# Stick-breaking values by pairs of heads in the two column halves of TensorE, with transposed outputs, and the group norm by partition sums right behind the heads

## The chip, the cores and the metric

The kernel runs on one core of one Trainium2 chip. The metric is the time of one execution on the device in microseconds (us), the median of several; less is better. All times below are us unless marked ns. The engines are TensorE (PE; its weight loads are shown apart as PEld), VectorE (DVE), ScalarE (ACT), GpSimd (POOL) and SyncE (SP), which issues the DMAs.

## The reference

Two transformer blocks, one behind the other, on 512 tokens of 1024 channels in fp32. The first block's mixer has four groups of 256 channels: a short convolution (group 0), a block-sparse attention with compressed tokens (NSA, group 1), a latent attention (MLA, group 2) and a stick-breaking attention of four heads of 64 (group 3). Each group is normalised by itself and all four go through one output projection. Only group 3 is touched:

```python
def stick_breaking_mixer(q, k, v):                       # 4 heads of 64
        z = jnp.einsum('bqhd,bkhd->bhqk', q_blk, k) * scale
        strict = kpos < (t0 + arange(Q_BLOCK))           # key before query
        log_1m = where(strict, log_sigmoid(-z), 0.0)
        rem = cumsum(log_1m, axis=3, reverse=True) - log_1m
        a = where(strict, exp(log_sigmoid(z) + rem), 0.0)
        return einsum('bhqk,bkhd->bqhd', a, v)
...
y = concatenate([y_a, y_b, y_c, y_d]).reshape(B, S, N_GROUPS, GROUP_WIDTH)
y = rms_norm(y, out_norm_w.reshape(N_GROUPS, GROUP_WIDTH))
x = x + y.reshape(B, S, D) @ w_out
```

## The kernel before

Everything stays in on-chip memory except the weights, which stream in on SP's queue (`wraw`, L268). A product of two fp32 matrices is mostly done as three matmuls on split operands (high and low part, L184, L185, L186; ACT makes a high part, L276 for weights and L192 for data, DVE the low part, L277 and L193). Some smaller products run as plain fp32 matmuls; each of those leaves two records in the trace.

A head of the stick-breaking group (`sb_head`, L960) has three steps. `first` makes the transposed logits, keys on partitions and queries along the free axis, causal part only, in three PSUM banks (L981, L982), and turns them into log terms: three passes of ACT (L987 to L989), one of DVE (L990), a causal select of POOL (L974), and a split (L192, L193, names `sbLh`, `sbLl`). `second` adds the running sums by matmuls with triangles (L1002) and takes the exponential (ACT, L1006, name `sba`; POOL's select again). `third` multiplies by the values: for each of the ten causal pairs of a query tile and a key tile, the 128x128 block of `sba` is the stationary operand and 64 columns of `svN` move (L1014), and ACT copies the result, tokens on partitions, into `yN` (L1016).

The loop over heads calls `second` of head h, `first` of head h+1, `third` of head h, and between them takes steps of a side generator: the projections of the values, of the NSA keys and values (L184 to L186 into `kvN`), and the hidden layer of the compressed tokens (`compress_hidden`), whose operand `cB` is made from `cv0` and `cv1` (DVE L1243, a split by ACT and DVE into `cB`) and consumed by the matmuls L1252 and L1254. `cv1` needs rows shifted by a DMA (L700). Behind the heads stand `group_stats` (squares with sums on ACT L853, a power on POOL L227, scaling on DVE L857) and `compress_out` (POOL copies `Tc` L1118, fed by a round trip to memory L1101, L1108; a norm with POOL's power `crs`, L227; DVE `ckn` L1290; PE L1295). The transposes of `yN` into `yT6` and `yT7` come later (`group_out`, L866). Lines L453 to L468 (`token_rs`, `token_bcast`) are the norm by partition sums that the convolution group has: four matmuls with a vector of ones, a power on POOL, diagonal tiles on DVE (L464), one matmul that spreads the factor over all partitions (L466), a copy, two multiplications.

The Python order is not the order of the program: a scheduler takes all instructions with their dependences and fixes one order for each engine. Each engine then works strictly in its order and waits where an operand is not there.

Of the kernel before, what the change touches and what calls it, by code (L numbers as in the profile page):

```python
# [22 lines left out]
P = 128  # L23
# [126 lines left out]
class Kern:  # L150
# [427 lines left out]
    def mixers1(self):  # L578
# [73 lines left out]
        with tc.tile_pool(name="mx", bufs=1) as mp:  # L652
# [28 lines left out]
            def ev_qv(t, b):  # L681
                nc.scalar.activation(qN[:, t, :], b[:, :256], AF.Copy, scale=nm.rs[:, t:t + 1])
                nc.vector.tensor_scalar(svN[:, t, :], b[:, 256:512], nm.rs[:, t:t + 1], None, op0=OP.mult)
            ySB = self.T(mp, [P, NT, 256], F32, "yN", 2)
            ncv = self.T(mp, [P, NT, 352], F32, "ncv")
            gN = self.T(mp, [P, NT, 12], F32, "ng", 1)
            xs = self.T(self.drp, [P, 8, S], F32, "xs", 1)
# [36 lines left out]
            def side2():  # L724
# [12 lines left out]
                        tc.keep_in_program_order(nc.sync.dma_start(xs[:, k, :], self.x[k]))  # L737
                        yield
                yield from self.along(self.conv(mp, nm, w), itertools.chain(self.mla_stats(mp, ncv), store()))
                self.group_out(ySB, 3, "pT")  # L740
                cq = self.mla_trans(mp, ncv)
                yield
                yield from self.mla_proj(mp, ncv, cq, st)
                yield from self.along(self.conv_gate(nm, w, st), self.mla_rope(mp, ncv, st["mla"]), 2)
                norm = self.conv_norm(st["acc"])
                for h in range(4):
                    hd.append(self.mla_head(h, st["mla"]))
                    yield
# [19 lines left out]
                    yield  # L768
            hd = []
            self.fq.append(side())  # L770
            heads = [self.sb_head(mp, h, sq[h], sk[h], svN, ySB) for h in range(4)]
            self.fill(10)
            heads[0][0]()
            self.fill(16)
            for h in range(4):
# [5 lines left out]
                    heads[h + 1][0]()  # L781
                heads[h][2]()
                self.fill(6)
            self.dbg("ySB", ySB)
            self.yH = [None] * 8
            for k in (2, 3):
                self.yT[k] = self.T(mp, [P, S], F32, f"yT{k}")
            self.drain()
            g2 = side2()
            self.fq = [self.weave(self.compress_out(mp, st), g2, 2), g2]  # L790
            self.group_stats(mp, ySB, 3)
            n = self.nsa_prep(mp, qN, st["kvN"])
            self.fill(8)
            self.fill(2)
            while "g" not in st:
                self.fill(1)
# [160 lines left out]
        self.nc.tensor.matmul(out, q[h][:, qs], k.hi[:, ks], start=True, stop=False)  # L957
        self.nc.tensor.matmul(out, q[h][:, qs], k.lo[:, ks], start=False, stop=True)  # L958

    def sb_head(self, mp, h, q, k, svN, ySB):  # L960

        nc = self.nc
        st = {}
# [3 lines left out]
        def R(kt, t, q0=None):  # L967
            o = 384 if kt == 3 else 0
            q0 = kt if q0 is None else q0
            return t[bank[kt]][:, o + (q0 - kt) * P: o + (NT - kt) * P]  # L970

        def causal(a, i):
            for o in ([0, 384] if i == 1 else [0]):
                nc.gpsimd.affine_select(out=a[:, o:o + P], in_=a[:, o:o + P], pattern=[[1, P]], compare_op=OP.is_gt,  # L974
                                        fill=0.0, base=0, channel_multiplier=-1)

        def first():
            st["z"] = z = [self.ps('L'), self.ps('L'), self.ps('pT')]
            for kt in (0, 1, 3, 2):
                ks = slice(kt * P, (kt + 1) * P)  # L980
                nc.tensor.matmul(R(kt, z), k.hi[:, ks], q[:, kt * P:S], start=(kt != 3), stop=False, skip_group_check=True)  # L981
                nc.tensor.matmul(R(kt, z), k.lo[:, ks], q[:, kt * P:S], start=False, stop=True, skip_group_check=True)  # L982
            st["hi"], st["lo"] = [], []
            for i in range(3):
                n = widths[i]
                e = self.T(mp, [P, 512], F32, "sbe", 3)[:, :n]
                nc.scalar.activation(e, z[i][:, :n], AF.Abs)  # L987
                nc.scalar.activation(e, e, AF.Exp, scale=-1.0)
                nc.scalar.activation(e, e, AF.Ln, bias=1.0)  # L989
                nc.vector.scalar_tensor_tensor(e, z[i][:, :n], 0.0, e, op0=OP.max, op1=OP.add)  # L990
                causal(e, i)
                hl = self.hl(mp, [P, 512], "sbL", 3)
                self.split(hl[:, :n], e)
                st["hi"].append(hl.hi)
                st["lo"].append(hl.lo)

        def second():
            z = st["z"]
            for kt in range(NT):
                for m, j in [(self.trir, kt)] + [(self.negr, j) for j in range(kt + 1, NT)]:  # L1000
                    for src in (st["hi"], st["lo"]):
                        nc.tensor.matmul(R(kt, z, j), m, R(j, src), start=False, stop=True, skip_group_check=True)  # L1002
            st["a"] = []
            for i in range(3):
                a = self.T(mp, [P, 512], F32, "sba", 3)
                nc.scalar.activation(a[:, :widths[i]], z[i][:, :widths[i]], AF.Exp)  # L1006
                causal(a, i)
                st["a"].append(a)

        def third():  # L1010
            ov = self.ps('o')[:, :256].rearrange("p (t d) -> p t d", t=NT)
            for qt in range(NT):
                for kt in range(qt + 1):
                    nc.tensor.matmul(ov[:, qt, :], R(kt, st["a"], qt)[:, :P], svN[:, kt, h * 64:(h + 1) * 64],  # L1014
                                     start=(kt == 0), stop=(kt == qt))
            nc.scalar.activation(ySB[:, :, h * 64:(h + 1) * 64], ov, AF.Copy)  # L1016
        return first, second, third

    def conv(self, mp, nm, w):
# [35 lines left out]
                nc.vector.tensor_add(acc, acc, sq)  # L1055
        yield from self.tproj_g(nm.H, w, [(0, 256)], ev_b)

    def conv_norm(self, acc):
        rs = self.token_rs(acc, S, 1.0 / 256, "L")
        yield  # L1060
        R = self.token_bcast(rs, S, "L")
        yield
        for c in range(2):
            self.nc.vector.tensor_mul(self.yT[c], self.yT[c], R)
        yield

    def nsa_norms(self, mp, qN, kvN):
# [993 lines left out]
```

## Time and profile before

| | before |
|---|---|
| median of 3 runs | 1604.54 (1604.54 to 1604.95) |
| the profiled execution | 1605.0, its span 1603.2 |
| mean granted clock of TensorE | 0.997 |
| PE busy | 1586.2, 99% of the span |
| DVE, ACT, POOL busy | 927.7, 678.8, 52.5 |

The span runs from the first to the last instruction in the trace; the execution's own time holds 1.8 more around it. The four heads and the work woven between them lie within the first 122 us of the span; the two tiles of transposes that the change removes are at 169 and 170. Behind that, the rest of the first block and all of the second are the same code before and after.

### The profile page before, as it was taken

The numbers are of one execution on the slowest core, as the hardware profiler recorded it, in microseconds if no ns is written. First come the engines' busy times: TensorE is split into PE (matmuls) and PEld (weight loads), VectorE is DVE, ScalarE is ACT, GpSimd is POOL, SyncE is SP. The second block draws the span as 40 slices with busy tenths as digits, with TensorE's granted clock in tenths as the row PEclk, the third lists the DMA queues.
The fourth block names the chain that finished last, engine by engine and source line by source line (L and its number), as shares of the span: only waits on it lengthen the run. The fifth ranks groups of instructions, "written<-read, shape, count | busy, mean of one in ns | idle before, by whom it ended". The sixth has DMA issues, their size and how long they took to land.

```text
span 1603.2 us, 20825 instructions
## 1 busy us (share of the span) xinstructions
PE 1586.2 (99%) x8075; PEld 1332.7 (83%) x8075; DVE 927.7 (58%) x1597; ACT 678.8 (42%) x1170; POOL 52.5 (3%) x99
## 2 busy tenths in 40 slices
PE   9999999999999999999999999999999999999998
PEld 7888878888888888888898777888988888888886
DVE  6666885644324433476666665674767556436662
ACT  5776654544213333344343366362544333213332
POOL 0121010000000000000000000000000000000000
PEclk9999999999999999999999999999999999999999
DMA  5243121223222232232222211333323233323331
GB/s 179 76 131 124 53 99 40 79 94 104 92 99 99 92 102 95 88 92 60 76 64 72 84 45 67 119 101 109 121 92 105 82 103 94 104 92 99 97 119 53
DMA packets 108134, 148.15 MB, mean 92 GB/s; under 512 B 7903, under 2 KB 58884, under 8 KB 108036
## 3 DMA queue, kind: packets, MB, share of 16 engines
q1 hardware_dynamic: 107892, 146.72, 28.6%
q8 instruction: 63, 1.03, 0.3%
q14 instruction: 35, 0.29, 0.1%
q10 hardware_dynamic: 144, 0.11, 0.0%
HBM read 142.31 MB, written 4.20 MB: 91 GB/s over the span
## 4 chain that ended last, share of the span: by engine, by line
PE 94%; DVE 4%; ACT 1%; POOL 1%; issue 1%; POOLq 0%; DVEq 0%; ACTq 0%
PE mm L184 27%; PE mm L186 27%; PE mm L185 26%; PE lv L1642 2%; PE o L912 1%; PE o L1685 1%; PE pT L901 1%; PE o L1815 1%; PE L L957 1%; PE pT L1792 1%; PE L L958 1%; DVE wlo L277 1%; PE o L184 0%; PE o L186 0%; PE o L185 0%
## 5 line engine op out<-in xcount | busy, mean ns | idle before, releaser
L277 DVE TENSOR_TENSOR wlo<-wraw,whi 128x1024 fp32r<-128x1024 f32 (+4 forms) x267 | 310.3, 1163 | 436.0 <-ACT whi L276 424.4
L276 ACT ACTIVATE whi<-wraw 128x1024 fp32r<-128x1024 f32 (+4 forms) x267 | 269.8, 1011 | 539.0 <-PE mm L185 472.6
L184 PE MATMUL mm<-H4h,whi 128*128 128x512 f32 x147 | 59.2, 403 | 0.0
L184 PE MATMUL mm<-H6h,whi 128*128 128x512 f32 x147 | 58.4, 401 | 0.4 <-ACT H6h L195 0.4
L184 PE MATMUL mm<-H7h,whi 128*128 128x512 f32 x147 | 58.3, 397 | 0.0
L488 DVE TENSOR_TENSOR x<-mm,x 128x512 f32<-128x512 f32 x72 | 48.8, 686 | 16.2 <-PE mm L186 15.7
L184 PE MATMUL mm<-H5h,whi 128*128 128x512 f32 x147 | 57.9, 394 | 0.0
L186 PE MATMUL mm<-H6h,wlo 128*128 128x512 f32 x147 | 57.7, 393 | 0.0
L185 PE MATMUL mm<-H7l,whi 128*128 128x512 f32 x147 | 57.7, 392 | 0.0
L185 PE MATMUL mm<-H6l,whi 128*128 128x512 f32 x147 | 57.7, 392 | 0.0
L186 PE MATMUL mm<-H4h,wlo 128*128 128x512 f32 x147 | 57.6, 392 | 0.0
L186 PE MATMUL mm<-H7h,wlo 128*128 128x512 f32 x147 | 57.4, 391 | 0.0
L185 PE MATMUL mm<-H4l,whi 128*128 128x512 f32 x147 | 57.3, 390 | 0.0
L186 PE MATMUL mm<-H5h,wlo 128*128 128x512 f32 x147 | 57.3, 390 | 0.0
L185 PE MATMUL mm<-H5l,whi 128*128 128x512 f32 x147 | 57.3, 390 | 0.0
L184 PE MATMUL mm<-H0h,whi 128*128 128x512 f32 x139 | 55.3, 398 | 0.0
L184 PE MATMUL mm<-H3h,whi 128*128 128x512 f32 x139 | 55.2, 397 | 0.0
L184 PE MATMUL mm<-H2h,whi 128*128 128x512 f32 x139 | 55.1, 397 | 0.0
L184 PE MATMUL mm<-H1h,whi 128*128 128x512 f32 x139 | 54.8, 394 | 0.0
L185 PE MATMUL mm<-H2l,whi 128*128 128x512 f32 x139 | 54.6, 392 | 0.0
L186 PE MATMUL mm<-H0h,wlo 128*128 128x512 f32 x139 | 54.5, 392 | 0.0
L186 PE MATMUL mm<-H2h,wlo 128*128 128x512 f32 x139 | 54.5, 392 | 0.0
(1300 smaller groups left out, 4190.4 us busy)
## 6 DMA issues: line engine op xcount, KB each, us to landing
wraw<-ffn_w_dram SPq DMA_DIRECT2D x64, 512.0 KB, 3.6
wraw<-w_up_dram SPq DMA_DIRECT2D x88, 256.0 KB, 2.9
wraw<-w_in_dram SPq DMA_DIRECT2D x35, 512.0 KB, 3.5
wraw<-w_down_dram SPq DMA_DIRECT2D x22, 512.0 KB, 3.6
wraw<-w_mem_kv_dram SPq DMA_DIRECT2D x16, 512.0 KB, 3.7
wraw<-w_in_dram SPq DMA_DIRECT2D x52, 128.0 KB, 2.3
wraw<-w_in_dram SPq DMA_DIRECT2D x22, 256.0 KB, 2.9
wraw<-cmp_w_dram SPq DMA_DIRECT2D x8, 512.0 KB, 4.7
```

Of the source, the lines that this page charges most:

```text
L184: mm(out, a.hi, b.hi, start=start, stop=False, skip_group_check=skip)
L185: mm(out, a.hi, b.lo, start=False, stop=False, skip_group_check=skip)
L186: mm(out, a.lo, b.hi, start=False, stop=stop, skip_group_check=skip)
L276: nc.scalar.activation(hi, raw, AF.Copy)
L277: nc.vector.tensor_sub(lo, raw, hi.bitcast(F32))
L488: self.nc.vector.tensor_add(self.x[k], b, self.x[k])
L901: nc.tensor.transpose(b[:, t * P:(t + 1) * P], st["p"][:, t * P:(t + 1) * P], self.ident)
L912: nc.tensor.matmul(o(), st["pT"][:, t * P:(t + 1) * P], v(t), start=(t == 0), stop=(t == nt - 1))
L957: self.nc.tensor.matmul(out, q[h][:, qs], k.hi[:, ks], start=True, stop=False)
L958: self.nc.tensor.matmul(out, q[h][:, qs], k.lo[:, ks], start=False, stop=True)
L1642: nc.tensor.matmul(b[:, t * P:(t + 1) * P], ym[:, t * P:(t + 1) * P], mix(X, c, t * P, P), start=True, stop=True)
L1685: nc.tensor.matmul(ov[:, t, :], Am[:, s_, t * P:(t + 1) * P], v[:, s_, h * P:(h + 1) * P], start=(s_ == 0), stop=(s_ == NT - 1))
```

## The change

The values are now computed for two heads at a time. The 64 columns of `svN` of a head are the stationary operand, and the head's `sba` moves: for each of the four key tiles one matmul of 512, 384, 256 or 128 columns, and the two heads write to the two halves of the partitions of one PSUM bank, so that the outputs are channels by tokens. The exponentials of the even heads stay in other buffers (`mla_p`) until the odd head is done. ACT copies the pair's bank into `yT6` or `yT7` and squares it into `nacc` or `nsq`; DVE adds the second square. The norm by partition sums (`conv_norm`, renamed `group_norm`) then runs on these right behind the heads. `group_stats` and `group_out` are gone for this group.

```diff
             def ev_qv(t, b):
...
-            ySB = self.T(mp, [P, NT, 256], F32, "yN", 2)
+            pair = {}
...
-                self.group_out(ySB, 3, "pT")
                 cq = self.mla_trans(mp, ncv)
...
-            heads = [self.sb_head(mp, h, sq[h], sk[h], svN, ySB) for h in range(4)]
+            heads = [self.sb_head(mp, h, sq[h], sk[h], svN, pair) for h in range(4)]
...
-            self.group_stats(mp, ySB, 3)
+            norm3 = self.group_norm(pair["acc"], (6, 7))
+            next(norm3)
             n = self.nsa_prep(mp, qN, st["kvN"])
+            next(norm3)
             self.fill(8)
+            next(norm3)
             self.fill(2)
...
-            st["a"] = []
+            a = pair[h] = [None] * 3
             for i in range(3):
-                a = self.T(mp, [P, 512], F32, "sba", 3)
-                nc.scalar.activation(a[:, :widths[i]], z[i][:, :widths[i]], AF.Exp)
-                causal(a, i)
-                st["a"].append(a)
+                a[i] = self.T(mp, [P, 512], F32, "sba" if h % 2 else "mla_p", 3)
+                nc.scalar.activation(a[i][:, :widths[i]], z[i][:, :widths[i]], AF.Exp)
+                causal(a[i], i)

         def third():
-            ov = self.ps('o')[:, :256].rearrange("p (t d) -> p t d", t=NT)
-            for qt in range(NT):
-                for kt in range(qt + 1):
-                    nc.tensor.matmul(ov[:, qt, :], R(kt, st["a"], qt)[:, :P], svN[:, kt, h * 64:(h + 1) * 64],
-                                     start=(kt == 0), stop=(kt == qt))
-            nc.scalar.activation(ySB[:, :, h * 64:(h + 1) * 64], ov, AF.Copy)
+            if h % 2 == 0:
+                return
+            o = self.ps('o')
+
+            def values(kt, j):
+                return nc.tensor.matmul(o[64 * j:64 * j + 64, kt * P:S],
+                                        svN[:, kt, (h - 1 + j) * 64:(h + j) * 64], R(kt, pair[h - 1 + j]),
+                                        start=(kt == 0), stop=(kt == 3), skip_group_check=True)
+            m = values(0, 1)
+            with self.tc.issue_after(m.ins):
+                values(0, 0)
+                for kt in (2, 1, 3):
+                    for j in range(2):
+                        values(kt, j)
+            c = 6 + h // 2
+            y = self.yT[c] = self.T(mp, [P, S], F32, f"yT{c}")
+            nc.scalar.activation(y, o, AF.Copy)
+            if h == 1:
+                pair["acc"] = self.T(self.sp, [P, S], F32, "nacc", 1)
+                nc.scalar.activation(pair["acc"], o, AF.Square)
+            else:
+                sq = self.T(self.sp, [P, S], F32, "nsq", 2)
+                nc.scalar.activation(sq, o, AF.Square)
+                nc.vector.tensor_add(pair["acc"], pair["acc"], sq)
```

The scheduler's order moves at three places. First TensorE at the end of head 1's `second`: this is what it did there before (L1002 is head 1, L981 and L982 are `first` of head 2, L1014 the values of head 1, L1252 the hidden layer of the compressed tokens).

```order
L1002 MATMUL L_676<-sbLl_704,cmatr_81 128x128
L981 MATMUL L_856<-sqk1h_365,sqk3h_405 128x512
L982 MATMUL L_856<-sqk1h_365,yT_88_406 128x512
L1014 MATMUL o_898<-svN_436,sba_800 128x64 x2
L981 MATMUL L_857<-sqk1h_365,sqk3h_405 128x384
...
L1014 MATMUL o_898<-svN_436,sba_803 128x64
L1014 MATMUL o_898<-svN_436,sba_800 128x64
L1252 MATMUL mm_764<-whi_742,cB_769 64x256
```

After, the same place has the compressed tokens' rows (now L1270, L1272; sixteen of them) straight behind head 1's last sum, and head 2's logits (now L982, L983) only behind those, mixed with the NSA projections, with the pair's eight value matmuls (L1016) behind them.

```order
L1002 MATMUL L_675<-sbLl_703,cmatr_81 128x128
L1270 MATMUL mm_751<-whi_729,cB_756 64x256
L1272 MATMUL mm_751<-wlo_730,cB_756 32x256
...
L184 MATMUL mm_818<-whi_798,H0h_125 128x256
L982 MATMUL L_843<-sqk1h_365,sqk3h_405 128x512
...
L983 MATMUL pT_845<-sqk1h_365,yT_88_406 128x256
L1016 MATMUL o_885<-sba_787,svN_436 64x512
L1016 MATMUL o_885<-mla_p_613,svN_436 64x512
L1016 MATMUL o_885<-mla_p_620,svN_436 64x256
L1016 MATMUL o_885<-sba_794,svN_436 64x256
```

So head 2's logits and the values no longer stand ahead of the rows that need `cB`. Second, VectorE at the same place, before and then after (`ev_765` and `ev_752` lead to the `cB` of those rows; `ev_1004` and `ev_992` come from `cv1`, the tile that the shift DMA L700 completes, and lead to the later `cB`).

```order
L277 TENSOR_TENSOR wlo_760<-wraw_758,whi_759 128x1024
L1243 TENSOR_TENSOR ev_765<-cv_132_648,vecs_75 128x8x31 x2
L193 TENSOR_TENSOR cB_769<-ev_765,cB_769 128x16x32
L1243 TENSOR_TENSOR ev_1004<-cv_133_649,vecs_75 128x8x31 x2
```

```order
L277 TENSOR_TENSOR wlo_747<-wraw_745,whi_746 128x1024
L193 TENSOR_TENSOR sbLl_713<-sbe_706,sbLh_712 128x256
L1261 TENSOR_TENSOR ev_752<-cv_131_647,vecs_75 128x8x31 x2
L1261 TENSOR_TENSOR ev_992<-cv_132_648,vecs_75 128x8x31
L193 TENSOR_TENSOR cB_756<-ev_752,cB_756 128x16x32
L1261 TENSOR_TENSOR ev_992<-cv_132_648,vecs_75 128x8x31
```

A row that needs the shift DMA now stands between `ev_752` and the low part of the first `cB`, and a weight's low part (`wlo_747`) ahead of head 1's last `sbLl`. Third, GpSimd behind the heads, before and then after (`grs` and `rs` are the powers of the group's norm, `crs` that of the compressed keys).

```order
L227 TENSOR_TENSOR grs_255_1261<-grs3t_1262,mhalf_80 128x4
L227 TENSOR_TENSOR crs_1374<-crst_1375,mhalf_80 32x1
L1118 COPY Tc_1290<-sba_1292 128x2x7
L1118 COPY Tc_1290<-sba_1292 128x2x15 x3
```

```order
L227 TENSOR_TENSOR rs_1235<-rst_1236,mhalf_80 128x4
L1136 COPY Tc_1260<-sba_1262 128x2x7
L1136 COPY Tc_1260<-sba_1262 128x2x15 x3
L1151 COPY ev_1330<-kvN_744 128x4x64
L1152 COPY ev_1330<-kvN_744 128x4x64
L1136 COPY Tc_1260<-sba_1276 128x2x7
L1136 COPY Tc_1260<-sba_1276 128x2x15 x3
L227 TENSOR_TENSOR crs_1344<-crst_1345,mhalf_80 32x1
```

The power `crs` has moved behind ten copies. On VectorE, the copy that feeds the round trip to memory (L1099 before, L1117 after) now stands behind the first diagonal tile (L464), which needs `rs`.

## Rows read from the trace of the kernel before

**Rows 1.** The page: busy time by engine, share of the span, instructions.

```profile
PE 1586.2 (99%) x8075; PEld 1332.7 (83%) x8075; DVE 927.7 (58%) x1597; ACT 678.8 (42%) x1170; POOL 52.5 (3%) x99
```

**Rows 2.** Windows: length, busy PE PEld DVE ACT POOL (records), clock, DMA share, GB/s.

```profile
74.30:77.62 3.32, 2.63 (x19) 2.06 (x18) 2.31 (x4) 2.26 (x5) 2.09 (x4) 1.00 0.80 237
77.62:105.00 27.38, 27.32 (x216) 25.29 (x216) 17.74 (x24) 22.29 (x42) 7.12 (x18) 1.00 0.42 133
110.00:122.00 12.00, 12.00 (x80) 10.52 (x79) 9.62 (x29) 8.38 (x26) 4.25 (x12) 1.00 0.42 131
```

**Rows 3.** Timeline, heads 0 and 1: start, length, engine, row, [idle before <-releaser].

```profile
63.76 0.39 PE L981 MATMUL L<-sqk0l,sqk2l 128*128 128x512 f32 x1
...
65.02 2.34 PE L1014 MATMUL o<-svN,sba 128*128 128x64 f32 x20
...
67.17 0.47 PE L184 MATMUL mm<-H4h,whi 128*128 128x512 f32 x1
...
71.53 0.45 PE L1002 MATMUL L<-sbLl,cmatr 128*128 128x384 f32 x1 [0.50 <-DVE sbLl L193]
...
73.00 0.39 PE L1002 MATMUL L<-sbLl,cmatr 128*128 128x256 f32 x1 [0.49 <-DVE sbLl L193]
...
73.70 0.56 SPq L700 DMA_DIRECT2D cv<-cv  x1
...
74.31 0.45 PE L981 MATMUL L<-sqk1h,sqk3h 128*128 128x512 f32 x1
...
76.62 0.69 DVE L193 TENSOR_TENSOR cB<-ev,cB 128x512 fp32r<-128x512 f32 x1 [0.70 <-ACT cB L192]
...
77.62 0.31 PE L1252 MATMUL mm<-whi,cB 128*64 128x256 f32 x1
...
78.61 1.11 DVE L1243 TENSOR_TENSOR ev<-cv,vecs 128x248 f32<-128x248 f32 x2 [1.30 <-DMA cv<-cv]
```

**Rows 4.** Timeline, the values of heads 2 and 3.

```profile
95.19 2.34 PE L1014 MATMUL o<-svN,sba 128*128 128x64 f32 x20
...
106.21 0.88 PE L1014 MATMUL o<-svN,sba 128*128 128x64 f32 x6 [0.28 <-POOL sba L974]
...
107.37 0.43 PE L1014 MATMUL o<-svN,sba 128*128 128x64 f32 x2 [0.28 <-POOL sba L974]
```

**Rows 5.** TensorE's timeline where the removed and the added forms stand elsewhere.

```profile
169.00 0.66 PE L866 MATMUL pT<-cmat,yN 128*128 128x128 f32 x4
169.49 0.27 PE L1335 MATMUL mm<-cmat,ncv 128*128 128x128 f32 x1
...
306.00 0.95 PE L453 MATMUL o<-ones,nacc 128*128 128x2 f32 x8
306.81 0.47 PE L184 MATMUL mm<-H2h,whi 128*128 128x512 f32 x1
...
313.93 1.02 PE L466 MATMUL o<-nsq,ones 128*128 128x512 f32 x2
...
943.96 1.31 PE L1815 MATMUL o<-wpT,qkv 128*64 128x128 f32 x20
945.20 0.55 PE L1792 MATMUL pT<-cmat,wp 128*128 128x128 f32 x3
```

**Rows 6.** Timeline behind the heads: POOL, ACT, PE.

```profile
118.77 0.73 POOL L227 TENSOR_TENSOR crs<-crst,mhalf 32x1 f32<-32x1 f32 x1 [3.76 <-DVE crst L210]
119.01 0.42 ACT L1112 ACTIVATE sbLh<-sba 128x256 f32<-128x256 f32 x1 [1.02 <-DMA sba<-scr]
...
119.47 2.21 POOL L1118 COPY Tc<-sba 128x14 f32<-128x14 f32 x8
...
121.69 0.24 PE L1295 MATMUL L<-cmat,ckn 32*128 32x32 f32 x1
```

**Rows 7.** Windows around a later stretch in which PE waits.

```profile
204.00:214.30 10.30, 8.13 (x62) 6.65 (x61) 10.24 (x27) 8.37 (x16) 0.54 (x1) 1.00 0.01 2
214.40:217.80 3.40, 3.40 (x19) 3.33 (x18) 3.40 (x7) 1.93 (x3) 0.00 (x0) 0.50 0.50 140
```

More of the change, by code (lines that the diff above doesn't have):

```diff
@@ L744, in side2 @@
                 yield from self.along(self.conv_gate(nm, w, st), self.mla_rope(mp, ncv, st["mla"]), 2)
-                norm = self.conv_norm(st["acc"])
+                norm = self.group_norm(st["acc"], (0, 1))
                 for h in range(4):
@@ L783, in mixers1 @@
                 self.fill(6)
-            self.dbg("ySB", ySB)
             self.yH = [None] * 8
@@ L958, in mm_pair, with sb_head @@
         self.nc.tensor.matmul(out, q[h][:, qs], k.lo[:, ks], start=False, stop=True)
-    def sb_head(self, mp, h, q, k, svN, ySB):
+    def sb_head(self, mp, h, q, k, svN, pair):
         nc = self.nc
@@ L982, in first @@
                 nc.tensor.matmul(R(kt, z), k.lo[:, ks], q[:, kt * P:S], start=False, stop=True, skip_group_check=True)
-            st["hi"], st["lo"] = [], []
+            st["hi"], st["lo"] = [None] * 3, [None] * 3
             for i in range(3):
@@ L993, in first @@
                 self.split(hl[:, :n], e)
-                st["hi"].append(hl.hi)
-                st["lo"].append(hl.lo)
+                st["hi"][i], st["lo"][i] = hl.hi, hl.lo
         def second():
@@ L1056, in conv_gate, with group_norm @@
         yield from self.tproj_g(nm.H, w, [(0, 256)], ev_b)
-    def conv_norm(self, acc):
+    def group_norm(self, acc, ks):
         rs = self.token_rs(acc, S, 1.0 / 256, "L")
@@ L1062, in conv_norm @@
         yield
-        for c in range(2):
-            self.nc.vector.tensor_mul(self.yT[c], self.yT[c], R)
+        for k in ks:
+            self.nc.vector.tensor_mul(self.yT[k], self.yT[k], R)
         yield
```

## The prediction

> **What bounds the kernel now.** I read the page first: TensorE (PE) is busy for 1586.2 of 1603.2 us [rows 1]. Nothing else is near it, so the time can change in two ways only: PE gets less or more to do, or it waits less or more. What it does behind the first 122 us is the same code before and after (apart from eight transposes), so all the rest of the span merely shifts, and the whole question is when PE gets through the heads.
>
> There I read the windows. From 77.62 to 105.00 PE is busy for 27.32 of 27.38 us and behind the heads for 12.00 of 12.00, while in the 3.32 us from 74.30 it is busy for 2.63 [rows 2]. The reader is to see that this stretch is full, but that something has to fill it: at the same time ACT is busy for 22.29 us of 27.38, because each head is a chain of ACT, DVE, POOL, ACT and DVE between two groups of matmuls. The timeline shows what filled it. The 20 records of head 0's values lie from 65.02 to 67.17, just behind the logits of head 1, where that head's chain has begun; even so PE then waits 0.50 and 0.49 for the last link of the chain, `sbLl` [rows 3]. Head 2's values are one row of 20 records at 95.19 in the same position under head 3's chain [rows 4]. The values were the cover.
>
> **PE's work.** Removed: 20 records in 67.17 - 65.02 = 2.15 us per head [rows 3], 8.6 for four; the two waits of 0.28 for POOL's selects inside head 3's values [rows 4], 0.56; and two groups of four transposes at (169.49 - 169.00) = 0.49 less about 0.05 for the change of form, 0.87 together [rows 5].
>
> Added, the norm: eight records L453 take 306.81 - 306.00 = 0.81; the two records L466 0.43 each, 0.86, since one of the two lasts 1.02 - 0.59 = 0.43 where 0.59 is the length of the other [rows 5].
>
> Added, the values: per pair 2 x (512 + 384 + 256 + 128) = 2560 moving columns. At L466's 0.86 for 512 that is 4.30 us if the two halves run one after the other. The window attention's L1815 has the same arrangement, 64-column outputs that alternate between two halves: 20 records of 128 columns in 945.20 - 943.96 = 1.24 us, 62 ns a record, where the transposes, whole-width and also 128 columns, need 0.49/4 = 0.12 a record [rows 5]. So the halves overlap, and a pair costs 4.30/2 = 2.15 and about 0.2 for entering and leaving the form. The second pair is cut by six other matmuls behind its third one, whose partner half is then empty: 0.43 more, and 0.2 for another change of form. Together 2 x 2.35 + 0.63 = 5.3; the bound on the other side, no overlap, is 5.3 + 4.3 = 9.6 [rows 5].
>
> Sum of the work: -8.6 - 0.56 - 0.87 + 0.81 + 0.86 + 5.3 = -3.1 us. The Trainium skill's page "TensorEngine Tiling (Array Packing)", section Performance Considerations, recommends exactly this: where the moving side has 64 columns or fewer, swap the sides and tile by columns, for up to twice the speed. By that rule alone the change pays, and L1815's 62 ns a record agree with it. What the rule leaves out is who stands behind the matmuls that become fewer.
>
> **PE's waits, place by place.**
>
> *Head 1's chain.* Without head 0's values PE is 2.15 us earlier at L1002, but the chain is no shorter: it begins with the logits, which end at 65.02 either way. PE already waited for its last links, so the whole 2.15 becomes a wait. A weight's low part of 1024 columns now stands ahead of the last `sbLl` on DVE; it is of the length of L1243's pair, 1.11 [rows 3], and I count half of it on the path, since that `sbLl` waits for its ACT part too (bounds 0 and 1.11). So head 1's sums end about 0.55 behind the 74.31 of before, at 74.85.
>
> *The first `cB`.* Before, the logits of head 2 and eight value records filled 74.31 to 77.62, until the low part of `cB` was there (from DVE at 76.62, 0.69 long) [rows 3]. After, the sixteen rows that need `cB` come first, and nothing fills. Moreover DVE now does a row of `cv1` before that low part, and the shift DMA for it was issued at 73.70 and had DVE waiting 1.30 until 78.61 [rows 3], 4.9 after issue. By the new order I put its issue about 1.1 earlier, at 72.6, since the tile's DVE product no longer waits behind `sbLl`; it lands at 76.5 to 77.5. With half of L1243's 1.11 and the 0.69 behind it, `cB` is ready at 77.7 to 78.8; I take 78.2, against 77.62. PE idles from 74.85 to then, 3.3 us, and still has head 2's logits to do that it had behind it before: 1.26, as head 1's took from 63.76 to 65.02 [rows 3].
>
> *Head 2's chain.* Its logits now come later, and cover for its chain are the rest of the logits behind the first two banks (about 0.6), the pair's block (2.35) and sixteen rows of 256 columns, 2.0 at the logits' 1.26 for 2560 columns. By ACT's new order nine instructions lead to the first `sbLh`: three passes for each of two banks, one of the third, the new copy of the pair, the split; ACT's 42 in the window take 0.53 each [rows 2], so 4.8, and DVE adds two of 0.69 [rows 3]. That is 6.2 against 4.95: a wait of 1.2, and I count 0.6 more for the two other banks, 1.8 in all; before, this window had 0.06 [rows 2]. Bounds: 0.5, where DVE's first part lies under ACT, and 2.5.
>
> *Head 3's chain.* The 20 records at 95.19 [rows 4] are gone from under it, and the pair's block comes behind the chain, not under it. That opens up to 2.15, and POOL's selects are waited for in the block as they were in the old values. I count 2.2; bounds 0.8 and 3.3.
>
> *Behind the heads.* Three things now hang on POOL: `rs` (a power like `crs`, 0.73, on more data), DVE's copy for the round trip to memory, which stands behind a diagonal tile that waits for `rs`, and `crs`, which stands behind the copies `Tc` (2.21 for eight). Before, `crs` ran at 118.77 and PE's L1295 at 121.69 without a stop, `Tc` behind it [rows 6]. The `Tc` copies wait for the round trip, whose end ACT awaited at 119.01 already [rows 6]. With the trip later by 0.7 or more and `crs` behind `Tc`'s 2.21 instead of ahead of it, from 119.0 on, L1295 is ready some 2.5 us later than it was; the new order puts about 1 us of other matmuls ahead of it, so 1.4 is left, and I count 0.6 more for a weight's low part that stands behind the same DVE row as the copy. Together 2.0; bounds 0.5 and 3.0.
>
> **The sum.** At the first `cB` matmul the new kernel stands 0.58 behind. From there: +1.26 (logits still to do), -5.6 (52 of the 80 value records at 2.15/20, the other 28 lay ahead of this point), -0.56, +5.3, +0.81, +0.86, -0.87, which is +1.2 for work; the waits +1.8, +2.2 and +2.0, which is 6.0. Together 0.6 + 1.2 + 6.0 = 7.8 us. The profiled execution was 1605.0, its span 1603.2 and 1.8 around it, and 0.46 over the median, so 1605.0 + 7.8 - 0.46 = 1612.3; I say 1612. What this costs is not the new work but the cover taken away: the copies and squares on ACT are nothing on ACT's own account, yet they stand in head 2's chain.
>
> **Rivals.**
>
> *Faster, by the work alone.* Only the waits before 77.62 are real, and they are made up because ACT, DVE and the DMAs run ahead meanwhile; then the sum of work, -3.1, is all: 1604.54 - 3.1 = 1601.4. This is what the page's rule amounts to. For it: from 77.62 to 105 the chains kept up, PE waited 0.06 [rows 2]. Against: PE waited twice with the cover in place [rows 3]. It decides when all waits from head 1 on come to so little that -3.1 is not eaten; my count of them is 7.8 + 3.1 = 10.9, and they would have to be under 3.1. Chance 0.12.
>
> *No change.* The waits of heads 2, 3 and behind are at their lower bounds, 0.5 + 0.8 + 0.5 = 1.8, and `cB` is ready no later than before: 1.2 + 1.8 = 3.0, which gives 1607.1; with a part of head 1's 2.15 regained, 1605 to 1606. Chance 0.17 for within 3.2 us, which is 0.2% and about what a measurement tells from no change.
>
> *Halves that don't overlap.* If fp32 matmuls with 512 columns run one behind the other, 4.3 more: 1616.3. Against: L1815 [rows 5], of the same kind with fewer columns. Chance 0.06.
>
> *The clock.* In a later stretch PE was busy for 8.13 of 10.30 us, and in the 3.40 us behind it the granted clock was 0.50, that is 1.2 instead of 2.4 GHz [rows 7]; at full clock 3.40 us of work would have been 1.7. The long wait before `cB` and those behind it could bring such a dip: +1.7 for each, 1613.7 to 1615.4. Against: the wait of 0.69 in 3.32 us before brought none [rows 2]. Chance 0.15.
>
> **How the numbers follow.** My forecast in its own form has 0.50; slower in all 0.71 (0.50 + 0.06 + 0.15), same 0.17, faster 0.12. With the waits at their upper bounds (8.8) the sum is 10.6, 1614.7; with a dip 1616.4. The range 1602.0 to 1616.5 leaves out most of the faster rival and the tail of the last two. Within my forecast alone it is 1608 to 1615.5.
>
> **What would show it.** In the new trace: L1016's pairs should start together, eight matmuls in some 2.2 us; PE idle for about 2 us for `sbLl` ahead of head 1's sums and for about 3 us ahead of the first L1270, with DVE waiting for the DMA of `cv`; waits for `sbLl` at head 2 and head 3; a wait of over 1 us for `ckn` behind the heads; behind 122 us the same rows, all shifted by the same 7 to 8 us. The prediction is wrong if the first L1270 starts at 77 or earlier, if the chains of heads 2 and 3 end before PE gets to them, or if a stretch far behind the heads changes its length.

## The result, and the profile after

The changed kernel takes 1614.19 us (median of 6, 1612.82 to 1614.93), against 1604.63 of the kernel before on the same chip (median of 6): ratio 1.0058, 95% interval 1.0048 to 1.0069, 9.6 us slower. The forecast was 1612.0, the range 1602.0 to 1616.5. The profiled execution took 1614.65, its span is 1612.8.

First the page of the changed kernel, busy time by engine.

```profile
PE 1588.0 (98%) x8029; PEld 1327.0 (82%) x8029; DVE 929.2 (58%) x1600; ACT 677.0 (42%) x1161; POOL 50.3 (3%) x99
```

TensorE has 46 records fewer than in [rows 1] and is not less busy: 1588.0 against 1586.2. Part of that is clock: a matmul is busy for longer at half clock (L1270: 0.41 at 0.50, 0.28 at 1.00). The windows show it (start and end, length, then busy time and records of PE, PEld, DVE, ACT and POOL, the granted clock, DMA share, GB/s).

```profile
68.92:73.60 4.68, 2.57 (x9) 1.31 (x9) 4.62 (x8) 3.48 (x6) 1.16 (x3) 1.00 0.25 62
73.60:77.90 4.30, 3.00 (x15) 2.54 (x13) 3.39 (x7) 1.68 (x4) 0.38 (x1) 0.50 0.83 237
77.90:83.90 6.00, 6.00 (x28) 5.56 (x29) 2.26 (x3) 2.00 (x4) 0.84 (x3) 0.51 0.17 46
83.90:91.21 7.31, 7.16 (x55) 5.41 (x54) 2.53 (x4) 5.45 (x11) 0.71 (x3) 1.00 0.43 135
91.21:112.00 20.79, 19.35 (x130) 15.88 (x130) 12.69 (x18) 15.75 (x29) 4.79 (x14) 1.00 0.42 125
214.34:224.64 10.30, 8.13 (x62) 6.66 (x61) 10.24 (x27) 8.38 (x16) 0.54 (x1) 1.00 0.00 0
224.74:228.14 3.40, 3.37 (x30) 3.04 (x30) 3.40 (x7) 2.15 (x5) 0.00 (x0) 1.00 0.57 145
```

Three things are to be seen. From 68.92 to 77.90, head 1's sums and the wait for `cB` behind them, PE has work for 5.57 of 8.98 us. From 73.60 to 83.90 the granted clock is 0.50 to 0.51, that is 1.2 GHz; the part from 77.90 on is full of work, so 6.00 us are spent on what 3.1 would do at full clock. And the last two windows answer to [rows 7]: the same stretch with the same waits, but no half clock behind it this time.

The timeline of the changed kernel has the waits of head 1 one by one (start, length, engine, row, idle time before it and what ended that).

```profile
68.92 0.49 PE L1002 MATMUL L<-sbLh,cmatr 128*128 128x512 f32 x1 [0.64 <-ACT sbLh L192]
...
70.19 1.20 DVE L277 TENSOR_TENSOR wlo<-wraw,whi 128x1024 fp32r<-128x1024 f32 x1
...
72.05 0.61 PE L1002 MATMUL L<-sbLl,cmatr 128*128 128x384 f32 x2 [0.65 <-DVE sbLl L193]
...
73.08 0.48 SPq L700 DMA_DIRECT2D cv<-cv  x1
73.08 1.23 DVE L277 TENSOR_TENSOR wlo<-wraw,whi 128x1024 fp32r<-128x1024 f32 x1
...
74.70 0.58 PE L1002 MATMUL L<-sbLl,cmatr 128*128 128x256 f32 x1 [0.71 <-DVE sbLl L193]
...
75.65 0.63 ACT L192 ACTIVATE cB<-ev 128x512 fp32r<-128x512 f32 x1 [2.45 <-DVE ev L1261]
...
76.53 0.58 DVE L1261 TENSOR_TENSOR ev<-cv,vecs 128x248 f32<-128x248 f32 x1 [0.91 <-DMA cv<-cv]
...
77.02 0.73 DVE L193 TENSOR_TENSOR cB<-ev,cB 128x512 fp32r<-128x512 f32 x1
...
77.90 0.45 PE L1270 MATMUL mm<-whi,cB 128*64 128x256 f32 x1 [0.59 <-DVE cB L193]
```

In the kernel before the same sums start at 70.00 and have two waits of 0.5 [rows 3]; here they start 1.1 earlier and have six waits of 0.31 to 0.71, 3.46 together, three of which the rows show. The low parts of two weights stand between the low parts of the sums on DVE, and the row of `cv1` between the two parts of `cB`, waiting 0.91 for its DMA.

The pair's matmuls, in the same timeline: two start 0.01 apart.

```profile
86.70 0.64 PE L1016 MATMUL o<-sba,svN 128*64 128x512 f32 x1
86.71 0.64 PE L1016 MATMUL o<-mla_p,svN 128*64 128x512 f32 x1
87.18 0.59 PE L1016 MATMUL o<-sba,svN 128*64 128x512 f32 x1
...
89.00 0.33 PE L1270 MATMUL mm<-whi,cB 128*64 128x256 f32 x1
```

From 86.70 to 89.00 is 2.30 for the first pair, where the old form took 2.15 for one head. The halves overlap.

And behind the heads, answering to [rows 6]:

```profile
120.99 1.02 POOL L227 TENSOR_TENSOR rs<-rst,mhalf 128x4 f32<-128x4 f32 x1 [7.27 <-DVE rst L210]
122.05 0.29 DVE L464 TENSOR_SCALAR nsq<-cmat,rs 128x128 f32<-128x128 f32 x1 [1.14 <-POOL rs L227]
122.25 0.54 DVE L1117 COPY ev<-pT 4x384 f32<-4x384 f32 x1
...
128.27 0.42 ACT L1130 ACTIVATE sbLh<-sba 128x256 f32<-128x256 f32 x1 [1.49 <-DMA sba<-scr]
...
131.18 0.54 POOL L227 TENSOR_TENSOR crs<-crst,mhalf 32x1 f32<-32x1 f32 x1
...
132.37 0.21 PE L1313 MATMUL L<-cmat,ckn 32*128 32x32 f32 x1 [1.32 <-DVE cvn L1311]
```

`rs` holds up the diagonal tile (`nsq`), that the copy for the round trip to memory (L1117), that the `Tc` copies on POOL, and these hold up `crs`. DVE's rows for `ckn` and `cvn` wait for `crs`, and PE waits 1.32 for them.

All in one view, the waits of PE from head 1's logits to 150 (releaser, us in total, times, longest):

```profile
PE L L1002 <- ACT sbLh L192: 2.2, 5, 0.6
PE L L1002 <- DVE sbLl L193: 1.9, 4, 0.7
PE L L1313 <- DVE cvn L1311: 1.3, 1, 1.3
PE mm L1270 <- DVE cB L193: 0.6, 1, 0.6
PE mm L185 <- DVE wlo L277: 0.6, 2, 0.4
PE mm L184 <- ACT whi L276: 0.5, 1, 0.5
```

### The profile page after: what moved, and what is told of

Its sections match the earlier page's. It is cut to its first block, busy times and chain, and to the rows that moved or that the text cites. A ratio compares the mean times of both kernels' runs of the same rounds, so it can differ in the third digit from the quotient of the medians.

```text
span 1612.8 us, 20721 instructions
## 1 busy us (share of the span) xinstructions
PE 1588.0 (98%) x8029; PEld 1327.0 (82%) x8029; DVE 929.2 (58%) x1600; ACT 677.0 (42%) x1161; POOL 50.3 (3%) x99
## 4 chain that ended last, share of the span: by engine, by line
PE 89%; DVE 3%; ACT 2%; POOL 1%; issue 1%; POOLq 0%; DVEq 0%; ACTq 0%
PE mm L186 25%; PE mm L184 25%; PE mm L185 25%; PE lv L1660 2%; PE o L913 1%; PE o L1703 1%; PE pT L902 1%; PE o L1833 1%; PE L L958 1%; PE pT L1810 1%; PE L L959 1%; PE o L184 0%; PE o L186 0%; PE o L185 0%; PE lv L1680 0%
## 5 line engine op out<-in xcount | busy, mean ns | idle before, releaser
L488 DVE TENSOR_TENSOR x<-mm,x 128x512 f32<-128x512 f32 x72 | 48.7, 686 | 16.2 <-PE mm L186 15.7
```

Source lines behind the costliest of these rows:

```text
L488: self.nc.vector.tensor_add(self.x[k], b, self.x[k])
```

## The experiments

Twelve kernels ran, in three groups, each beside the kernel before on the same chip; its median was 1605.07 beside e1 to e4, 1604.94 beside e5 to e8 and 1604.78 beside e9 to e12. A difference to before is taken from these. All keep the computation whole; the first adds work that nobody reads. In the table "late" is the norm put later, "pinned" and "halfway" are two places for the DVE rows that read the shifted tile.

| kernel | median us | ratio to before, 95% interval |
|---|---|---|
| changed kernel | 1614.19 | 1.0058 (1.0048 to 1.0069) |
| e1, covers added | 1617.08 | 1.0075 (1.0062 to 1.0088) |
| e2, unpaired values | 1610.22 | 1.0034 (1.0021 to 1.0046) |
| e3, norm late | 1611.85 | 1.0044 (1.0031 to 1.0058) |
| e4, first pair undone | 1610.94 | 1.0040 (1.0027 to 1.0053) |
| e5, shift rows pinned | 1614.41 | 1.0063 (1.0050 to 1.0075) |
| e6, before, pinned | 1608.01 | 1.0020 (1.0011 to 1.0029) |
| e7, e4 + late + pinned | 1611.41 | 1.0038 (1.0025 to 1.0052) |
| e8, e2 + late + pinned | 1610.11 | 1.0032 (1.0019 to 1.0045) |
| e9, before, shift rows halfway | 1605.87 | 1.0004 (0.9996 to 1.0013) |
| e10, unpaired, late, halfway | 1608.19 | 1.0021 (1.0012 to 1.0029) |
| e11, second pair, late, halfway | 1608.22 | 1.0020 (1.0011 to 1.0029) |
| e12, both pairs, late, halfway | 1610.89 | 1.0037 (1.0024 to 1.0051) |

**e1: covers added.** For the even heads the old twenty records run again, into the bank that the pair overwrites:

```diff
+            o = self.ps('o')
             if h % 2 == 0:
+                ov = o[:, :256].rearrange("p (t d) -> p t d", t=NT)
+                for qt in range(NT):
+                    for kt in range(qt + 1):
+                        nc.tensor.matmul(ov[:, qt, :], R(kt, pair[h], qt)[:, :P], svN[:, kt, h * 64:(h + 1) * 64],
+                                         start=(kt == 0), stop=(kt == qt))
                 return
-            o = self.ps('o')
```

> The changed kernel with twenty value records in the old form added for head 0 and twenty for head 2, written to the bank that the pair overwrites later, read by nobody: 4.3 us of matmuls that do no useful work, in the two places under the chains of heads 1 and 3 from which the change took the old values. Theory (the heads are bound by the chains of ACT, DVE and POOL, and PE's time there is free as long as it stays a cover): no slower than the changed kernel, 1614 within 1 us; and if the stretch at half clock that begins at 73.6 in the changed kernel comes from the waiting ahead of it, it goes and the time falls by up to 3.0, to 1611. Rival (PE's work is what counts, and the added norm and forms are the loss): 4.3 us slower, 1618.5.

It came out between the two and outside of the theory's 1 us: 2.4 us over the changed kernel by the differences to before (12.0 against 9.6). The trace shows that the two places behave in opposite ways (first the timeline, then a window from head 2's sums to the end of head 3's):

```profile
65.80 2.34 PE L1016 MATMUL o<-svN,mla_p 128*128 128x64 f32 x20
...
70.97 0.68 DVE L697 TENSOR_TENSOR cv<-mm,R 64x512 f32<-64x512 f32 x1 [0.89 <-PE mm L186]
...
74.48 0.48 SPq L700 DMA_DIRECT2D cv<-cv  x1
...
79.53 0.57 DVE L1266 TENSOR_TENSOR ev<-cv,vecs 128x248 f32<-128x248 f32 x1 [2.51 <-DMA cv<-cv]
...
80.89 0.44 PE L1275 MATMUL mm<-whi,cB 128*64 128x256 f32 x1 [2.18 <-DVE cB L193]
...
104.48 2.34 PE L1016 MATMUL o<-svN,mla_p 128*128 128x64 f32 x20
```

```profile
93.76:114.75 20.99, 20.54 (x148) 17.93 (x149) 12.69 (x18) 15.65 (x29) 3.94 (x14) 1.00 0.37 103
```

In the second place 2.15 us of dead work cost 0.2: the window is 20.99 long, and 20.79 in the changed kernel. There the theory holds. In the first place the dead records stand ahead of the twelve matmuls that lead to `cv0` and `cv1`. Now DVE waits 0.89 for those, the shift DMA goes out at 74.48 in place of 73.08, the row of `cv1` waits 2.51 for it, and the first `cB` matmul comes at 80.89 in place of 77.90. Of these 3.0, 0.4 is there from head 1's logits on; 1.0 is the later issue; the other 1.6 is the DMA itself, whose reader starts 5.05 behind its issue and started 3.45 behind it in the changed kernel. Why the DMA took longer was not tested. So PE's time is not free there: it is on the way to a DMA that `cB` waits for by DVE's order. The half clock stayed (75.5 to 85.9).

**e2, e3 and e4: one part undone.** In e2 each head's values run at once, in the head's own column half:

```diff
-            if h % 2 == 0:
+            j = h % 2
+            o = pair["o"] = self.ps('o') if j == 0 else pair["o"]
+            for kt in (0, 2, 1, 3):
+                nc.tensor.matmul(o[64 * j:64 * j + 64, kt * P:S],
+                                 svN[:, kt, h * 64:(h + 1) * 64], R(kt, pair[h]),
+                                 start=(kt == 0), stop=(kt == 3), skip_group_check=True)
+            if j == 0:
                 return
```

> The changed kernel with the values of each head in the new form (64-column stationary, transposed output, norm behind the heads) but at once behind that head, each in its own column half, so that no two halves run together. PE has about 2.15 us per head to do as in the old form. Theory (the loss is the cover and the order): head 2's logits stand ahead of the rows that need cB again, no half clock at 74 to 84, waits of heads 1 to 3 as before; what remains is about 1.6 of work (norm, entering and leaving the form) and 2.4 of waits behind the heads: 1608.5, between 1607 and 1610. Rival (the transposed form and its norm are the loss themselves): with 4.3 us more work than the changed kernel 1614 or above.

In e3 the norm's three steps move:

```diff
-            norm3 = self.group_norm(pair["acc"], (6, 7))
-            next(norm3)
             n = self.nsa_prep(mp, qN, st["kvN"])
-            next(norm3)
             self.fill(8)
-            next(norm3)
...
+                norm3 = self.group_norm(pair["acc"], (6, 7))
+                next(norm3)
                 cq = self.mla_trans(mp, ncv)
                 yield
+                next(norm3)
+                next(norm3)
```

> The changed kernel with only the steps of the stick-breaking group's norm put later, where the transposes stood before (behind the convolution's loop). Theory: the wait for ckn behind the heads (1.3) and that for a weight's low part there (0.4) go, the half clock and the heads' waits stay: 1612.3, between 1611.5 and 1613. Rival (the norm's place is of no account, since something else is late there): 1614 within 0.7.

e4 takes the branch of e2 for heads 0 and 1 and the changed kernel's for heads 2 and 3.

> The changed kernel with heads 0 and 1 as in the run on unpaired values, heads 2 and 3 still as a pair, norm still right behind the heads. Theory: the half clock goes with the first pair's waits, and most of the loss with it; the second pair's waits (1.7) and those behind the heads (2.4) stay, its saved work of about 1.4 counts: 1608, between 1606.5 and 1609.5. Rival (both pairs cost alike): half of the 9.6 stays, and the norm: 1610.5 or above.

e3 came out as the theory said, 1611.85: the wait for `ckn` is gone, and 2 to 3 us of the loss belong to the norm's place. e2, at 1610.22, is just above the theory's range and far from the rival's 1614; the order ahead of `cB` is that of before, but a stretch of half clock came at 83.2 that I had said would go. e4, at 1610.94, lies outside of the theory's range and in the rival's: undoing the first pair takes off 3 to 4 us of the 9.6 and not most of it. The rival's reason does not hold either: undoing the second pair too (e2) takes off another 0.7 only, which is within the spread of the two kernels, so most of what e4 and e2 lose is not the pairing. (e4's profiled execution took 1613.06, the slowest of its five.) The timelines of e2 (first two rows) and e4 (last two) show what I had not counted:

```profile
79.67 1.07 DVE L1255 TENSOR_TENSOR ev<-cv,vecs 128x248 f32<-128x248 f32 x2 [2.00 <-DMA cv<-cv]
...
82.11 0.39 PE L185 MATMUL mm<-wlo,H0h 128*128 128x256 f32 x1 [1.97 <-DVE wlo L277]
```

```profile
79.82 1.08 DVE L1269 TENSOR_TENSOR ev<-cv,vecs 128x248 f32<-128x248 f32 x2 [1.94 <-DMA cv<-cv]
...
82.28 0.39 PE L185 MATMUL mm<-wlo,H0h 128*128 128x256 f32 x1 [1.92 <-DVE wlo L277]
```

DVE waits two us for the shift DMA with the low part of PE's next weight behind it, and PE waits as long for that. In the kernel before DVE waited 1.30 there [rows 3], and head 1's remaining value records stood ahead of that weight on PE.

**e5 to e8: the shift rows pinned.** The two additions that read the shifted tile are kept behind all DVE work traced before them:

```diff
-                nc.vector.tensor_add(blk[:, 8 * half:8 * half + 8, 0:31], v, ps.unsqueeze(2).to_broadcast([P, 8, 31]))
+                add = nc.vector.tensor_add(blk[:, 8 * half:8 * half + 8, 0:31], v,
+                                           ps.unsqueeze(2).to_broadcast([P, 8, 31]))
+                if t:
+                    self.tc.keep_in_program_order(add)
```

> The changed kernel with one change of order: the two DVE rows that read the shifted cv1 tile are pinned behind the DVE work traced before them, so that the low part of the first cB no longer stands behind a row that waits for the shift DMA; TensorE's order up to head 3 is the same. Theory (the wait ahead of the first cB matmul is set by that DMA row): in the changed kernel cB's high part was there at 76.28 and its low part at 77.75 with the DMA wait between; so the first L1270 comes at 77.0 in place of 77.9, and 1613.3 for the whole (0.9 less), or 1610.5 if with the shorter wait the half clock goes too. Rival (cB is late for another reason): no change, 1614.2 within 0.5.

> The kernel before with the same pin. There DVE waited 1.30 for the shift DMA too, but TensorE had head 1's values to do meanwhile and was busy 27.32 of 27.38. Theory (a wait under a cover is free): no change, 1604.6 within 1.0. Rival (the DMA wait on DVE costs in any order): about 1 us faster or more, 1603.5 or below.

> The run with the first pair undone, with the norm put late and the shift rows pinned as well: three repairs together. In that run TensorE waited 1.92 for a weight's low part behind the shift DMA row, 1.07 for a weight's high part soon after, and 1.3 and 0.4 behind the heads. Theory (these waits are all of order, none of the form): all go, 1610.9 - 2.3 - 3.0 = 1605.6, between 1604.5 and 1607. Rival (new waits take their place, since ACT and DVE have no slack in the heads): 1608 or above.

> The run with unpaired values, with the norm put late and the shift rows pinned. It has 1.4 us more matmul work than the run with only the first pair undone, but head 2's values stand under head 3's chain as a cover. Theory: the wait of 1.97 and the stretch of half clock at 83 that followed go, 1610.2 - 2.0 - 1.5 - 0.4 = 1606.3, between 1605 and 1607.5, and the waits of head 3 are smaller than in the other run by about what the work is larger. Rival: as there, 1608 or above.

All four missed the theory: 1614.41, 1608.01, 1611.41, 1610.11. e5 has the time of its rival, but not for the rival's reason; e7 and e8 lie where theirs said, since a new wait came; e6 was slower, which neither side had said. The pin was too strong. In e5 the wait ahead of the first `cB` matmul did go (76.93, no idle time before it), but all four now make the second `cB` only when head 3's logits are done, and PE waits for it:

```profile
76.93 0.44 PE L1273 MATMUL mm<-whi,cB 128*64 128x256 f32 x1
...
101.43 0.47 PE L1273 MATMUL mm<-whi,cB 128*64 128x256 f32 x1 [3.48 <-DVE cB L193]
```

This gave the cleanest test of the cover. Timelines of e7, then of e8:

```profile
97.02 0.33 PE L1281 MATMUL mm<-whi,cB 128*64 128x256 f32 x1 [3.48 <-DVE cB L193]
```

```profile
93.99 2.37 PE L1014 MATMUL o<-sba,svN 128*64 128x512 f32 x8
...
97.55 0.33 PE L1267 MATMUL mm<-whi,cB 128*64 128x256 f32 x1 [1.20 <-DVE cB L193]
```

The place is the same: e8's trace is 0.5 later than e7's from head 1's logits on, and here too. Where head 2's values stand under the wait (e8) PE waits 1.20, where they don't (e7, and e5 with the same 3.48) it waits 3.48. The difference of 2.28 is the length of the values, 2.37: work there costs nothing, and work saved there gains nothing. e6 waits 1.33 with the old values in that place. The test is in the rows and not in the medians of e7 and e8: e7's five executions run from 1608.99, the profiled one, with a mean granted clock of 0.999, to 1611.56 with 0.995.

**e9 to e12: the same repairs for all, and only the pairing varied.** The additions are now traced halfway through the first `cB`'s units and pinned there (in DVE's order that is behind the weights that PE needs first), and the norm is late in e10 to e12.

```diff
+                if t == 0 and u == 1:
+                    blk = shifted(1, AV, 1)
```

> The kernel before with the rows that read the shifted cv1 tile traced halfway through the first cB's units and pinned there, so that they stand behind the weights' low parts that TensorE needs first, and not as late as in the earlier pin. It is the base for the three kernels beside it, which have the same rows in the same place. Theory (in the kernel before the DMA wait lies under head 1's values): no change, 1604.9 within 1.0. Rival (the DMA row costs in any order): 1603.5 or below.

> Unpaired values in the new form, norm late, shift rows halfway: every head's values are a cover for the next head's chain, as before. From the run on unpaired values (1610.2): the wait of 1.97 behind the DMA row goes, the half clock behind it (1.7) too, and 0.4 behind the heads: 1606.3, between 1605 and 1607.5. Rival (the transposed form and its norm are the loss): 1609 or above.

> The same with heads 2 and 3 as a pair: 1.4 us less matmul work than the unpaired run, and head 3's chain without head 2's values under it. Theory (cover): the work saved is given back as waits at head 3's sums (1.7 in the changed kernel), so within 1 us of the unpaired run, 1606.6. Rival (work): 1.4 faster than the unpaired run.

> The same with both pairs, that is the changed kernel with the norm late and the shift rows halfway: 3.5 us less matmul work than the unpaired run. Theory (cover): head 1's chain is bare, TensorE waits some 4 us at its sums, and half clock follows at 70 to 81; so it is the slowest of the three, 1610.5, between 1609 and 1612. Rival (work): the fastest of the three, 2 to 3.5 faster than the unpaired run.

The windows run from head 1's logits to the first row of the compressed attention (L1188, L1202 and L1194), for e10, e11 and e12, one fence each; the last fence has the part of e12 at half clock.

```profile
63.72:143.13 79.41, 76.85 (x469) 62.60 (x468) 51.92 (x107) 58.10 (x131) 19.89 (x44) 1.00 0.51 153
```

```profile
64.08:143.69 79.61, 76.00 (x469) 61.86 (x467) 52.45 (x107) 57.88 (x131) 17.51 (x44) 1.00 0.51 153
```

```profile
63.90:146.12 82.22, 76.79 (x468) 63.03 (x467) 51.75 (x107) 57.98 (x131) 15.93 (x44) 0.96 0.48 148
```

```profile
72.70:79.85 7.15, 6.38 (x31) 5.84 (x32) 3.80 (x7) 2.90 (x6) 1.10 (x4) 0.55 0.54 162
```

With one pair the stretch is as long as with none (79.61 and 79.41; medians 1608.22 and 1608.19), though PE has less to do. With two it is 2.8 longer, and the median is 2.7 higher; the executions of e12 (1610.32 to 1611.45) and e11 (1607.30 to 1608.75) do not overlap. That the second pair gains nothing and the first one costs is the theory's, and the opposite of the rival's. The sizes were 0.4 to 2 us too low: e12 is inside its range, e11 as far from e10 as said, but e10 lies outside of its range and below its rival's 1609, since I had counted on the unpaired kernel to come nearer to the kernel before. e9 is the kernel before within its noise. No version beat the kernel before.

Waits alone do not make e12 slower than e11. PE is idle for 5.43 us of e12's stretch and for 3.61 of e11's, 1.8 more. Its busy time is 0.8 more, although it has fewer matmuls to run: 6.38 us of it ran at 0.55 of the clock, which would be 3.5 at full clock, so about 2.9 is clock, and the work itself fell by about 2.1. By this estimate the waits give back about what the pairing saved, as for the second pair, and the loss is about as large as the half clock. e10 and e11 had no half clock in this stretch. No run had the first pair's waits at full clock, so it stays open how much of the 2.9 would then be waiting.

What e10 costs over e9, 2.3 us, is the new form and its norm without any pairing: by my terms 0.8 for entering and leaving the form and 0.81 + 0.86 for the norm, less 0.87, is 1.6; the rest was not told apart.

The differences to before give the parts of the 9.6, each uncertain by one to two us by the intervals: 3.5 for the norm's place and the order of the shift rows (changed kernel to e12), 2.7 for the first pair (e12 to e11), nothing for the second (e11 to e10), 2.3 for the form (e10 to e9), and 1.1 of e9 that is not clear of noise.

## Why the prediction was right, and where it was not

*What bounds the stretch.* Right, and shown by e8 against e7, by the second place of e1 and by e10 against e11: in the heads PE waits for the chains of ACT and DVE, and values taken out from under a chain return as a wait of about the same length. But that accounts for the gain that did not come. It is not the whole of the 9.6: "not the new work but the cover taken away" leaves out the form's own 2.3 and the clock, and the norm's place costs by another chain.

*PE's work.* The terms for the pairs held. The first pair took 2.30 where I had 2.35, and its rows stand some 0.2 further from their neighbours on the two sides together than rows of one form do, as I had put in; L1016's halves overlap, so the rival without overlap (1616.3) falls. The rule of the Trainium skill's page "TensorEngine Tiling (Array Packing)", section Performance Considerations, agrees with the trace for the matmuls themselves (8.6 us of values became about 5.2) and says nothing of the time of this kernel.

*Head 1's chain and the first `cB`.* I had 78.2 for the first `cB` matmul and it came at 77.90, with all of the trace 0.35 later from the start, so 0.6 earlier than forecast. The way there differed: the sums did not end at 74.85 but near 77.3, because six waits for DVE and ACT and, from 73.6, the half clock stretched them. So the wait of about 3 us that I had named as a sign ahead of the first L1270 was 0.59, and that of about 2 for the sums was 3.46: the time of the first `cB` was near, and the way PE spent the time until then was not as I had told it.

*The clock.* This is the term that the likeliest case lacked. I had it as a rival at 0.15, with 1.7 for a dip. Here 6.00 us of full work ran at 0.51, an estimated loss of 2.9, and the rival's 1613.7 to 1615.4 is where the time lies. The two stretches of half clock of the kernel before, of which [rows 7] shows one, were absent. That gave back only half a microsecond: the offset between the two traces, 10.3 at the window of [rows 7], is 9.84 at L466 (313.93 in [rows 5]).

```profile
323.77 1.02 PE L466 MATMUL o<-nsq,ones 128*128 128x512 f32 x2
```

The very dip from which I took the 1.7 cost nothing in the end. From the end of the waits of [rows 7] to the same later row of DVE (L488), the kernel before, with half clock, and the changed kernel, without, take the same time for the same records:

```profile
214.30:232.81 18.51, 18.25 (x97) 14.94 (x97) 15.62 (x30) 9.33 (x20) 4.40 (x1) 0.91 0.51 170
```

```profile
224.64:243.12 18.48, 17.25 (x97) 13.21 (x97) 15.62 (x30) 9.12 (x20) 4.40 (x1) 1.00 0.53 171
```

PE was busy for 1.0 longer and idle for 1.0 less: there it would have waited anyhow. Behind 77.90 in the changed kernel head 2's logits stand among and behind the slow rows and its chain begins with them, which is why I count the 2.9 in full; no run shows it by itself.

*The waits at heads 2 and 3.* Counted 1.8 and 2.2. The profile calls 0.59 and 0.76 idle there. Rows behind a wait are also further apart than rows without one (0.33 behind the row of 512 columns at 91.94, 0.23 elsewhere); with that the starts give, as an estimate against the kernel before, about 1.1 and 1.7. Both are inside the bounds and below my sizes.

*Behind the heads.* Counted 2.0: 1.4 for `ckn` and 0.6 for a weight. Measured idle 1.32 and 0.37, by the very chain from `rs` to `crs`. e3 confirmed the sum: 2.2 by the ratios, 2.8 by the differences to before.

*The sum.* The stretch from head 1's logits to the first row of the compressed attention grew by 10.0 (78.10 to 88.10). My 7.8, less 0.6 at `cB` and about 1.2 at heads 2 and 3, plus 2.9 of half clock, is 8.9. About 1 us stays unassigned; half of it is the last row of the stretch, for which PE waits 0.77 here and 0.24 in the kernel before. The 1612 against 1614.19 is thus a right mechanism with one missing term that smaller waits partly hid, and that the number came as near is in part luck.

*The signs.* Behind the heads the rows are shifted by 10.3 and later by 9.6, not by 7 to 8; the steps are where the clock differed. That stretches far behind changed their length I had named as a sign of being wrong, and it came, by 0.4 at most in one place. Three of my sums off the forecast took the 0.46 off twice: the lower bounds of the waits give 1607.5 and not 1607.1, the upper ones 1615.1 and not 1614.7, with a dip 1616.8 and not 1616.4, which is outside of my range.

*What I did not see* is how much the shift DMA governs. I priced it as a part of the first `cB`. The repairs showed that DVE's row behind it sits ahead of other operands too (1.97 in e2, 1.92 in e4), and that PE's work ahead of `cv0` and `cv1` moves it (e1). Its own time is not fixed: 3.4 from issue to landing in the changed kernel, 4.9 in the kernel before, 5.0 in e1 and 5.6 in e2.

## What to carry to other kernels

Before a matmul is made cheaper, look at what the engine does next: if the next row waits for a chain of other engines that began earlier, the saved time is a wait there, and the test is to add dead work in that place and see whether the time moves. Nothing else may hang behind the place, as the DMA did in e1. Where a scheduler fixes the order, an edit in one place reorders rows far from it; a row that waits for a DMA belongs behind whatever the busy engine needs first, but not behind everything. The norm's place cost here as much as the first pair, since a copy on DVE, and through it a power on POOL, stood behind it in queues that are worked in order. And half clock cost nothing where PE would have waited anyhow [rows 7], so the length of such a stretch is not its price.

## What the hardware showed that I had not expected

The granted clock fell in the changed kernel at 73.6, while PE was waiting on and off, 2.57 busy of the 4.68 us before, with no single wait over 0.65. It stayed at 0.50 until 83.8, and from 77.90 on PE was full. The same stretch of waits, 8.13 busy of 10.30, was followed by half clock in the kernel before [rows 7] and by full clock in the changed one. e2 and e4 had the same wait of almost 2 us at 80; e2's clock fell at 83.2 and e4's stayed full until 180.7. One program does not settle it either: e7's five executions took 1608.99 and 1609.58 with a mean granted clock of 0.999 and 0.998, and 1611.41 to 1611.56 with 0.995 and 0.996. So a stretch of waits alone did not tell whether half clock follows; what does was not settled here.
